# Second mixer: keys and queries projected pair by pair around the third gated projection and the first attention

## The chip, the core and the metric

One core of one Trainium2 chip runs the whole program. The metric is the time of one execution on the device in microseconds (us). The engines are TensorE (PE in the rows, its weight loads PEld), VectorE (DVE), ScalarE (ACT), GpSimd (POOL) and SyncE (SP, which here only issues transfers). Each engine runs its own instructions strictly in order and waits on semaphores for the others.

## What is computed

Two sequences of 256 tokens (width 1024) go through two layers, each a mixer and a convolutional feed-forward part, each followed by a layer norm. The first layer's mixer is a neighbourhood attention with a spatial gate. The change is in the second layer's mixer, which joins latent attention (8 heads, here 4 pairs) with a gated 31-tap convolution over 512 channels (here 4 groups of 128):

```python
def latent_attention(c_q, c_kv, k_rope_in, q_norm_g, w_uq, kv_norm_g, w_ukv, cos, sin):
    q = (rmsnorm(c_q, q_norm_g) @ w_uq).reshape(B, S, MLA_HEADS, MLA_NOPE + MLA_ROPE)
    q_nope, q_rope = jnp.split(q, [MLA_NOPE], axis=-1)
    q_rope = apply_rope(q_rope, cos[:, None, :], sin[:, None, :])
    kv = (rmsnorm(c_kv, kv_norm_g) @ w_ukv).reshape(B, S, MLA_HEADS, MLA_NOPE + MLA_V)
    k_nope, v = jnp.split(kv, [MLA_NOPE], axis=-1)
...
        s = (jnp.einsum('bqhd,bkhd->bhqk', qn_i, k_nope)
             + jnp.einsum('bqhr,bkr->bhqk', qr_i, k_rope)).astype(jnp.float32) * scale
        p = jax.nn.softmax(s, axis=-1).astype(v.dtype)
        return jnp.einsum('bhqk,bkhd->bqhd', p, v)

def odd_mixer(...):
    h = x @ w_in
    c_q, c_kv, k_r, glu_a, glu_g = jnp.split(h, [o1, o2, o3, o4], axis=-1)
    c = latent_attention(c_q, c_kv, k_r, ...)
    d = glu_a * jax.nn.sigmoid(glu_g)
    d = jax.nn.silu(layernorm(dwconv(d, conv_w, conv_b), conv_ln_g, conv_ln_b))
    return jnp.concatenate([c, d], axis=-1) @ w_out
```

## The kernel before

All 512 tokens stay on chip. Every fp32 product with a weight is made of three fast matmuls: the weight is split into a rounded half `whi` (a cast on ScalarE, L109) and the rest `wlo` (a subtraction on VectorE, L111), and the activations likewise (L115, L116). All of these matmuls are issued by one helper, L95, so the rows are told apart by tile names.

`odd_mixer` is written as a row of calls, and a list scheduler, which works with estimated durations, turns them into the fixed order of each engine; the order of the calls sets the priorities. The calls are:

- `glu(i)`, i from 0 to 3: the gated projection of one channel group, 2 times 24 matmuls into two PSUM banks, then its gate: a sigmoid on ScalarE (L551), the product into `dpad` on VectorE (L554), and the first tap of the convolution. The 31 taps of a group are shared out: 1 + 20 on VectorE (`cacc`, L557 and L719, accumulating in a PSUM bank) and 10 as products on ScalarE (`pr`, L559 and L723) that GpSimd adds up (L724); L725 adds both halves. From group 2 on, the gate also reloads ScalarE's table for the exponential.
- `cproj()` and `chain()`: the latent vectors, their norms, transposed to `cT`.
- `kvproj()`: v for the four blocks of tokens (`v1`, 4 times 3 matmuls, copied by ScalarE), then k of the four pairs (`k1`, 4 times 3 matmuls, copied by ScalarE into `kT`).
- `qproj()`: for each pair 6 matmuls for the rope half (evacuated by VectorE, L655) and 6 for the plain half (by ScalarE, L661), into `qT`.
- `attend(p)`: for each of two sequences and two heads (16 such steps in all, four to a pair; a step is called a head below) the scores `s`, the row maximum (DVE L491), two exponentials with their sums (ACT L494), a reciprocal (DVE L497), the scaling (ACT L501; in the last pair DVE L503), four transposes `pt` on TensorE and their copy to `PTr` (ACT, in the last pair DVE, L510), then the product with V (`pv`) and its split into `mixT`.

The calls stand in the order `glu(0)`, `cproj`, `chain`, `glu(1)`, `kvproj`, `qproj`, `glu(2)`, `attend(0)`, `attend(1)`, `glu(3)`, `attend(2)`, `attend(3)`; then the output projection's first half (`op0`, `dn1` banks), the convolution's taps, its layer norm (transposes `ct`, statistics, `cnm`, transposes back `cb`), and the projection's second half.

The exponentials are written to a ring of two tiles `er`, which is four half tiles, taken from the pool of large activation tiles. A second pool, `tp`, has eight temporaries of 2 KB per partition, among them the gates' sigmoids.

Of the kernel before, what the change touches and what calls it, by code (L numbers as in the profile page):

```python
# [11 lines left out]
AF = mybir.ActivationFunctionType  # L12
# [3 lines left out]
P = 128  # L16
# [3 lines left out]
T = 512  # L20
# [29 lines left out]
def tile_encoder(ctx: ExitStack, tc: tile.TileContext, I, O):  # L50
# [17 lines left out]
    def act(shape, dt=F32, s="a"):  # L68
        return actp.tile(shape, dt, tag="act", name=nm(s))
# [7 lines left out]
    class Ring:  # L77
# [6 lines left out]
        def get(self):  # L84
            j = self.i % (2 * len(self.t))
            self.i += 1
            return self.t[j // 2][:, j % 2, :].rearrange("p (a k) -> p a k", a=2)

    def bank(pool, s="ps"):
        return pool.tile([P, 512], F32, tag="b", name=nm(s))  # L90
# [441 lines left out]
    def odd_mixer(xT):  # L532
# [40 lines left out]
        G = {"start": last_mm[0]}  # L573
# [63 lines left out]
        def qproj():  # L637
            cT = G["cT"]
            wq = G["wq"]
            ropeT = G["kr"][:, 1:2, 0:S].broadcast_to([P, 2, S])  # L640
            qT = G["qT"] = [act([P, 2, T], s="qT") for _ in range(4)]

            def qfeat(pool, c):
                ps = bank(pool, "q")
                for k in range(2):
                    wh, wl = wq[k][0][:, c * P:(c + 1) * P], wq[k][1][:, c * P:(c + 1) * P]
                    mm(ps, wh, cT[k][:, 0, :], k == 0, False)
                    mm(ps, wh, cT[k][:, 1, :], False, False)
                    mm(ps, wl, cT[k][:, 0, :], False, k == 1)
                return ps  # L650
            for p in range(4):
                ps = qfeat(pB, 4 + p)
                for h in (0, 1):
                    rows = slice(64 - 64 * h, 128 - 64 * h)
                    nc.vector.tensor_tensor(out=qT[p][rows, h, :].rearrange("p (s t) -> p s t", s=2),  # L655
                                            in0=ps[rows].rearrange("p (s t) -> p s t", s=2), in1=ropeT[rows],
                                            op=ALU.mult)
                ps = qfeat(pC, p)
                for h in (0, 1):
                    rows = slice(64 * h, 64 * h + 64)  # L660
                    nc.scalar.activation(out=qT[p][rows, h, :], in_=ps[rows], func=AF.Copy, scale=96 ** -0.5)  # L661

        def kvproj():
            cT = G["cT"]
            wkv = G["wkv"]
            V = G["V"] = [wp.tile([P, 2, 512], F32, tag="w", name=nm("V1")) for _ in range(2)]
            for t in range(NT):
                ps = bank(pB, "v1")
                gemm_tok([ps], cT[2], t, wkv[0], wkv[1], [slice(512, 1024)], True, True)
                nc.scalar.copy(out=V[t // 2][:, t % 2, :], in_=ps)  # L670
            kT = G["kT"]
            for p in range(4):
                ps = bank(pC, "k1")
                wh, wl = wkv[0][:, p * P:(p + 1) * P], wkv[1][:, p * P:(p + 1) * P]
                mm(ps, wh, cT[2][:, 0, :], True, False)
                mm(ps, wh, cT[2][:, 1, :], False, False)
                mm(ps, wl, cT[2][:, 0, :], False, True)
                for h in range(2):
                    rows = slice(64 * h, 64 * h + 64)
                    nc.scalar.copy(out=kT[p][rows, h, :], in_=ps[rows])  # L680

        def attend(p):
            if p == 0:
                G["ring"] = Ring(2, "er"), Ring(2, "PTr")
            er, PTr = G["ring"]
# [16 lines left out]
        kvproj()  # L702
        qproj()
        glu(2)
        attend(0)
        attend(1)
# [215 lines left out]
```

## Time and profile before

| | us |
|---|---|
| median of the three runs | 1104.36 (1104.05 to 1105.21) |
| the profiled execution | 1104.76 |
| its span, first to last instruction | 1102.9 |
| TensorE busy | 1082.3 |
| VectorE busy | 673.2 |
| ScalarE busy | 488.7 |
| GpSimd busy | 226.6 |

The profiled execution is one run of its own. Busy times are sums over the span and say nothing of single stages; a matmul's end is modelled, since matmuls overlap. The second mixer lies between about 555 and 727 us.

### The profile page before, as it was taken

The numbers are of one execution on the slowest core, as the hardware profiler recorded it, in microseconds if no ns is written. First come the engines' busy times: TensorE is split into PE (matmuls) and PEld (weight loads), VectorE is DVE, ScalarE is ACT, GpSimd is POOL, SyncE is SP. The second block draws the span as 40 slices with busy tenths as digits, with TensorE's granted clock in tenths as the row PEclk, the third lists the DMA queues.
The fourth block names the chain that finished last, engine by engine and source line by source line (L and its number), as shares of the span: only waits on it lengthen the run. The fifth ranks groups of instructions, "written<-read, shape, count | busy, mean of one in ns | idle before, by whom it ended". The sixth has DMA issues, their size and how long they took to land.

```text
span 1102.9 us, 13655 instructions
## 1 busy us (share of the span) xinstructions
PE 1082.3 (98%) x5210; PEld 900.8 (82%) x5210; DVE 673.2 (61%) x996; ACT 488.7 (44%) x783; POOL 226.6 (21%) x222
## 2 busy tenths in 40 slices
PE   9999999999999999999999979999999999999996
PEld 7888778988888888888898856899888888888885
DVE  5378955766565656422578999587665656542227
ACT  5436644544444444421266797355444444431110
POOL 0482001200000000005464661830000000000173
PEclk9999999999999999999999979999999999999999
DMA  7852223533333323645232104254333333222602
GB/s 256 244 141 77 60 103 107 163 105 96 96 96 96 96 96 99 206 166 180 80 122 58 38 20 153 66 172 122 100 96 96 96 96 96 96 96 96 215 34 76
DMA packets 36098, 124.21 MB, mean 113 GB/s; under 512 B 4289, under 2 KB 5057, under 8 KB 36033
## 3 DMA queue, kind: packets, MB, share of 16 engines
q1 hardware_dynamic: 28864, 100.05, 29.5%
q0 software_dynamic: 6448, 22.53, 6.0%
q8 instruction: 41, 0.67, 0.3%
q10 hardware_dynamic: 720, 0.75, 0.2%
q14 instruction: 25, 0.20, 0.1%
HBM read 113.88 MB, written 8.39 MB: 111 GB/s over the span
## 4 chain that ended last, share of the span: by engine, by line
PE 93%; DVE 3%; ACT 2%; issue 1%; DMA 0%; POOL 0%; POOLq 0%; DVEq 0%; ACTq 0%
PE up L95 44%; PE dn L95 29%; PE qk L95 4%; PE op L95 4%; PE glu L95 3%; PE v L95 2%; PE u L95 2%; PE s L95 1%; PE pv L95 1%; PE pt L508 1%; DVE cacc L719 1%; PE lnT L237 1%; DVE wlo L111 1%; DVE qT L655 0%; ACT er L494 0%
## 5 line engine op out<-in xcount | busy, mean ns | idle before, releaser
L95 PE MATMUL up<-xT,whi 128*128 128x512 f32 (+1 forms) x1536 | 439.9, 371 | 0.0
L111 DVE TENSOR_TENSOR wlo<-raw,whi 128x1024 fp32r<-128x1024 f32 (+1 forms) x174 | 238.8, 1374 | 297.4 <-ACT whi L109 296.1
L95 PEld LDWEIGHTS up<-xT,whi 128*128 128x128 f32 x1536 | 279.9, 188 | 49.9
L109 ACT CAST whi<-raw 128x1024 fp32r<-128x1024 f32 (+1 forms) x174 | 182.4, 1050 | 249.1 <-PE dn L95 132.6
L95 PE MATMUL up<-xT,wlo 128*128 128x512 f32 (+1 forms) x768 | 284.0, 372 | 0.0
L95 PE MATMUL dn<-whi,gT 128*128 128x512 f32 x704 | 217.4, 389 | 0.0
L95 PEld LDWEIGHTS up<-xT,wlo 128*128 128x128 f32 x768 | 144.4, 188 | 24.9
L95 PEld LDWEIGHTS dn<-whi,gT 128*128 128x128 f32 x704 | 132.0, 188 | 27.2
L95 PE MATMUL dn<-wlo,gT 128*128 128x512 f32 x352 | 136.9, 389 | 0.0
L186 POOL DMA_DIRECT2D xres<-xscr x12 | 6.5, 546 | 576.0 <-PE dn L95 576.0
L95 PEld LDWEIGHTS dn<-wlo,gT 128*128 128x128 f32 x352 | 66.1, 188 | 13.8
L115 ACT CAST gT<-cv 128x512 fp32r<-128x512 f32 x44 | 27.3, 620 | 111.6 <-DVE cv L782 111.6
L771 ACT ACTIVATE cv<-up,par 128x512 f32<-128x512 f32 x88 | 68.3, 776 | 0.0
L774 DVE SCALAR_TENSOR_TENSOR cv<-up,par,cv 128x510 f32<-128x510 f32 x88 | 65.8, 748 | 2.7
L781 ACT ACTIVATE cv<-cv 128x512 f32<-128x512 f32 x44 | 27.8, 632 | 85.2 <-DVE cv L774 85.2
L772 DVE SCALAR_TENSOR_TENSOR cv<-up,par,cv 128x510 f32<-128x510 f32 x88 | 65.4, 743 | 0.0
L719 DVE SCALAR_TENSOR_TENSOR cacc<-dpad,par,cacc 128x512 f32<-128x512 f32 x80 | 58.9, 750 | 1.1
L724 POOL TENSOR_TENSOR acc<-acc,pr 128x512 f32<-128x512 f32 x36 | 48.7, 1353 | 38.9 <-ACT pr L723 32.2
L116 DVE TENSOR_TENSOR gT<-cv,gT 128x512 fp32r<-128x512 f32 x44 | 30.4, 692 | 27.5 <-ACT gT L115 27.5
L95 PE MATMUL op<-whi,mixT 128*128 128x512 f32 x128 | 44.3, 402 | 0.0
L95 PE MATMUL dn<-whi,mixT 128*128 128x512 f32 x128 | 42.8, 394 | 0.0
L95 PE MATMUL glu<-xT,khi 128*128 128x512 f32 (+1 forms) x160 | 42.0, 349 | 0.0
(195 smaller groups left out, 1351.4 us busy)
## 6 DMA issues: line engine op xcount, KB each, us to landing
raw<-in_wup SPq DMA_DIRECT2D x88, 512.0 KB, 3.6
raw<-in_wdn SPq DMA_DIRECT2D x44, 512.0 KB, 3.5
raw<-in_wout SPq DMA_DIRECT2D x16, 512.0 KB, 3.7
xscr<-xres POOLq DMA_DIRECT2D x12, 512.0 KB, 3.7
xres<-xscr POOLq DMA_DIRECT2D x12, 512.0 KB, 4.4
raw<-in_wqk SPq DMA_DIRECT2D x8, 512.0 KB, 6.6
raw<-in_wglu SPq DMA_DIRECT2D x8, 512.0 KB, 3.8
raw<-in_wug SPq DMA_DIRECT2D x7, 512.0 KB, 3.6
```

The source lines that it names most:

```text
L95: last_mm[0] = nc.tensor.matmul(out=out, lhsT=lhsT, rhs=rhs, start=first, stop=last)
L109: nc.scalar.copy(out=hi[:, :n], in_=raw[:, :n])
L111: nc.vector.tensor_tensor(out=lo[:, :n], in0=raw[:, :n], in1=hi[:, :n].bitcast(F32), op=ALU.subtract)
L115: nc.scalar.copy(out=dst[:, 0, sl], in_=src)
L116: nc.vector.tensor_tensor(out=dst[:, 1, sl], in0=src, in1=dst[:, 0, sl].bitcast(F32), op=ALU.subtract)
L237: nc.tensor.transpose(self.banks[k // 2][:, (k % 2) * S + q * P:(k % 2) * S + q * P + P], x[:, k * P:(k + 1) * P], ident)
L719: nc.vector.scalar_tensor_tensor(out=a, in0=dpad[i][:, :, j:j + S], scalar=pc("cw", i * 32 + j), in1=a, op0=ALU.mult, op1=ALU.add)
L724: nc.gpsimd.tensor_tensor(out=a2, in0=a2, in1=pr, op=ALU.add)
L771: nc.scalar.activation(out=c, in_=pv, func=AF.Identity, scale=pc(fw, ch * 4 + 1), bias=pc(fw, ch * 4 + 3))
L772: nc.vector.scalar_tensor_tensor(out=c[:, :, 1:S], in0=pv[:, :, 0:S - 1], scalar=pc(fw, ch * 4), in1=c[:, :, 1:S], op0=ALU.mult, op1=ALU.add)
L774: nc.vector.scalar_tensor_tensor(out=c[:, :, 0:S - 1], in0=pv[:, :, 1:S], scalar=pc(fw, ch * 4 + 2), in1=c[:, :, 0:S - 1], op0=ALU.mult, o ...
L781: nc.scalar.activation(out=cg, in_=cg, func=AF.Silu)
```

## The change

`qproj` and `kvproj` are taken apart. `kqproj(p)` projects k and q of one pair, with the same matmuls and evacuations; `vproj()` is what is left of `kvproj`. The pairs 0 and 1 are projected ahead of v and of the third gated projection, the pairs 2 and 3 behind the first pair's attention. The exponentials are no longer written to the ring `er` but each to a new tile of the pool of temporaries (`Loose`). Nothing else is changed; line numbers move by 3 or 4.

```diff
+    class Loose:
+        def get(self):
+            return tmp([P, 512], s="e").rearrange("p (a k) -> p a k", a=2)
...
-        G = {"start": last_mm[0]}
+        G = {"start": last_mm[0], "qT": [None] * 4}
...
+        def kqproj(p):
+            cT, wkv, kT = G["cT"], G["wkv"], G["kT"][p]
             ropeT = G["kr"][:, 1:2, 0:S].broadcast_to([P, 2, S])
+            qT = G["qT"][p] = act([P, 2, T], s="qT")
+            ps = bank(pC, "k1")
...
+            for h in range(2):
+                rows = slice(64 * h, 64 * h + 64)
+                nc.scalar.copy(out=kT[rows, h, :], in_=ps[rows])
+            ps = qfeat(pB, 4 + p)
...
+            ps = qfeat(pC, p)
...
         def attend(p):
             if p == 0:
-                G["ring"] = Ring(2, "er"), Ring(2, "PTr")
-            er, PTr = G["ring"]
+                G["ring"] = Ring(2, "PTr")
+            er, PTr = Loose(), G["ring"]
...
         glu(1)
-        kvproj()
-        qproj()
+        kqproj(0)
+        kqproj(1)
+        vproj()
         glu(2)
         attend(0)
+        kqproj(2)
+        kqproj(3)
         attend(1)
         glu(3)
```

What the scheduler makes of it shows in the built order. In the rows of an order, `name<-operands` are tiles with their numbers, `x2` is two such instructions in a row; the after version's line numbers are 3 or 4 higher.

TensorE where the first scores stand (`s`; `glu_5193` and `glu_5194` are the fourth gated projection, L95 is every matmul). Before:

```order
L95 MATMUL glu_5193<-xT_4277,klo_3991 128x512
L95 MATMUL glu_5193<-xT_4282,khi_3989 128x512 x2
L95 MATMUL glu_5193<-xT_4282,klo_3991 128x512
L95 MATMUL glu_5193<-xT_4287,khi_3989 128x512 x2
L95 MATMUL s_5027<-kT_4684,qT_4884 128x256 x2
L95 MATMUL glu_5193<-xT_4287,klo_3991 128x512
L95 MATMUL glu_5194<-xT_4252,khi_3995 128x512 x2
L95 MATMUL glu_5194<-xT_4252,klo_3997 128x512
L95 MATMUL s_5028<-kT_4684,qT_4884 128x256 x2
```

After (`glu_4911` is the third gated projection, `v_788` the last block of v, `glu_5197` the fourth gated projection):

```order
L99 MATMUL v_788_4905<-whi_4568,cT_4682 128x512
L99 MATMUL glu_4911<-xT_4282,khi_3893 128x512 x2
L99 MATMUL glu_4911<-xT_4282,klo_3895 128x512
L99 MATMUL glu_4911<-xT_4287,khi_3893 128x512 x2
L99 MATMUL glu_4911<-xT_4287,klo_3895 128x512
L99 MATMUL s_4973<-kT_4684,qT_4838 128x256 x2
L99 MATMUL s_4974<-kT_4684,qT_4838 128x256 x2
L99 MATMUL glu_5197<-xT_4252,khi_3989 128x512 x2
```

The first scores have moved ahead of the whole fourth gated projection and of half of the q and k projections.

ScalarE around the fourth gate's sigmoid (`sig`). Before (`er_5018<-s_5027` and `<-s_5028` are the exponentials of the first two heads, `er_5019<-s_5063` of the third):

```order
L494 ACTIVATE er_5018,rs_5050<-s_5028,nmx_5048 128x256 x2
L501 ACTIVATE er_5018<-er_5018,ri_5053 128x256 x2
L551 ACT_TABLE_LOAD
L551 ACTIVATE sig_5243<-glu_5194 128x512
L510 COPY PTr_5022<-pt_5042 128x512
L559 ACTIVATE acc_705_4425<-dpad_4421,par 128x512
L723 ACTIVATE pr_4428<-dpad_4421,par 128x512 x2
L494 ACT_TABLE_LOAD
L494 ACTIVATE er_5019,rs_5071<-s_5063,nmx_5069 128x256 x2
```

After (`e_5158` belongs to the seventh head, `e_5174` to the eighth):

```order
L505 ACTIVATE e_5129<-e_5129,ri_5135 128x256 x2
L498 ACTIVATE e_5158,rs_5161<-s_5152,nmx_5159 128x256 x2
L113 CAST whi_5765<-raw_5763 128x1024
L119 CAST mixT_4972<-pv_5145 128x256
L505 ACTIVATE e_5158<-e_5158,ri_5164 128x256 x2
L514 COPY PTr_4968<-pt_5139 128x512
L498 ACTIVATE e_5174,rs_5177<-s_5153,nmx_5175 128x256
L555 ACT_TABLE_LOAD
L555 ACTIVATE sig_5247<-glu_5198 128x512
L498 ACT_TABLE_LOAD
L498 ACTIVATE e_5174,rs_5177<-s_5153,nmx_5175 128x256
```

The sigmoid has moved from behind the second head to the middle of the eighth.

VectorE around the fourth gate's product (`dpad_4421`). Before (`cacc_5015` holds the third group's taps, `cacc_5248` the fourth's):

```order
L497 RECIPROCAL ri_5053<-rs_5050 128x2
L719 SCALAR_TENSOR_TENSOR cacc_5015<-dpad_4418,par,cacc_5015 128x512 x2
L554 TENSOR_TENSOR dpad_4421<-glu_5193,sig_5243 128x2x256
L491 TENSOR_REDUCE nmx_5069<-s_5063 128x2
L719 SCALAR_TENSOR_TENSOR cacc_5015<-dpad_4418,par,cacc_5015 128x512
L557 TENSOR_SCALAR cacc_5248<-dpad_4421,par 128x512
L719 SCALAR_TENSOR_TENSOR cacc_5015<-dpad_4418,par,cacc_5015 128x512
L719 SCALAR_TENSOR_TENSOR cacc_5248<-dpad_4421,par,cacc_5248 128x512
L719 SCALAR_TENSOR_TENSOR cacc_5015<-dpad_4418,par,cacc_5015 128x512
```

After (`cacc_4965` holds the third group's taps, `acc_705` takes its sum, `cacc_5252` is the fourth's):

```order
L722 SCALAR_TENSOR_TENSOR cacc_4965<-dpad_4418,par,cacc_4965 128x512 x2
L115 TENSOR_TENSOR wlo_5369<-raw_5365,whi_5367 128x1024
L728 TENSOR_TENSOR acc_705_4425<-cacc_4965,acc_705_4425 128x512
L501 RECIPROCAL ri_5135<-rs_5132 128x2
L495 TENSOR_REDUCE nmx_5159<-s_5152 128x2
L115 TENSOR_TENSOR wlo_5761<-raw_5757,whi_5759 128x1024
L501 RECIPROCAL ri_5164<-rs_5161 128x2
L495 TENSOR_REDUCE nmx_5175<-s_5153 128x2
L115 TENSOR_TENSOR wlo_5767<-raw_5763,whi_5765 128x1024
L120 TENSOR_TENSOR mixT_4972<-pv_5145,mixT_4972 128x256
L558 TENSOR_TENSOR dpad_4421<-glu_5197,sig_5247 128x2x256
L501 RECIPROCAL ri_5180<-rs_5177 128x2
```

The third group's taps have all moved ahead of the fourth gate's product, and weight differences (`wlo`) stand in between.

## Rows read from the trace of the kernel before

**Rows 1.** The page: the span, and each engine's busy time and share.

```profile
span 1102.9 us, 13655 instructions
...
PE 1082.3 (98%) x5210; PEld 900.8 (82%) x5210; DVE 673.2 (61%) x996; ACT 488.7 (44%) x783; POOL 226.6 (21%) x222
```

**Rows 2.** Stretches: window, busy us per engine, granted clock, DMA share and GB/s.

```profile
645.00:650.00 5.00, 2.13 (x5) 1.23 (x5) 4.59 (x9) 4.97 (x11) 2.48 (x3) 0.50 0.01 2
650.00:655.00 5.00, 4.34 (x13) 2.42 (x15) 5.00 (x10) 5.00 (x14) 4.53 (x4) 0.50 0.02 3
655.00:660.00 5.00, 5.00 (x25) 3.56 (x22) 5.00 (x11) 4.65 (x14) 3.01 (x4) 0.70 0.00 0
```

**Rows 3.** TensorE in order of time: start, length, instruction, [idle before, releaser].

```profile
631.09 1.02 PE L95 MATMUL s<-kT,qT 128*128 128x256 f32 x4
...
647.50 2.07 PE L95 MATMUL s<-kT,qT 128*128 128x256 f32 x4 [6.20 <-ACT er L494]
...
689.97 0.60 PE L508 MATMUL pt<-ident,er 128*128 128x128 f32 x4
```

**Rows 4.** Longer stretches, columns as in rows 2.

```profile
621.99:646.41 24.42, 19.31 (x90) 15.93 (x88) 22.50 (x37) 20.78 (x36) 14.88 (x11) 0.96 0.15 43
...
598.67:690.57 91.90, 83.10 (x400) 63.47 (x398) 86.46 (x155) 75.77 (x171) 41.75 (x38) 0.93 0.24 75
690.57:726.97 36.40, 36.38 (x174) 29.39 (x175) 20.94 (x33) 13.87 (x20) 23.92 (x12) 1.00 0.30 94
```

**Rows 5.** The chain of waits: start, length, engine and instructions.

```profile
602.23 4.08 PE glu L95 x18
```

**Rows 6.** ScalarE in order of time, columns as in rows 3.

```profile
613.25 1.20 ACT L661 ACTIVATE qT<-q 64x512 f32<-64x512 f32 x2
...
621.99 0.60 ACT L551 ACTIVATE sig<-glu 128x512 f32<-128x512 f32 x1 [0.16 <-PE glu L95]
...
639.59 0.91 ACT L501 ACTIVATE er<-er,ri 128x256 f32<-128x256 f32 x2 [0.23 <-DVE ri L497]
640.51 1.28 ACT L551 ACT_TABLE_LOAD   x1
641.81 0.60 ACT L551 ACTIVATE sig<-glu 128x512 f32<-128x512 f32 x1
...
643.80 1.32 ACT L723 ACTIVATE pr<-dpad,par 128x512 f32<-128x512 f32 x2
...
646.43 0.47 ACT L494 ACTIVATE er<-s,nmx 128x256 f32<-128x256 f32 x1
...
647.34 1.04 ACT L109 CAST whi<-raw 128x1024 fp32r<-128x1024 f32 x1
648.28 0.59 ACT L510 COPY PTr<-pt 128x512 f32<-128x512 f32 x1
...
664.60 0.47 ACT L494 ACTIVATE er<-s,nmx 128x256 f32<-128x256 f32 x1
```

**Rows 7.** VectorE in order of time, columns as in rows 3.

```profile
602.53 9.46 DVE L719 SCALAR_TENSOR_TENSOR cacc<-dpad,par,cacc 128x512 f32<-128x512 f32 x12
...
634.05 0.68 DVE L491 TENSOR_REDUCE nmx<-s 128x2 f32<-128x512 f32 x1
...
642.44 0.69 DVE L554 TENSOR_TENSOR dpad<-glu,sig 128x512 f32<-128x512 f32 x1 [1.41 <-ACT sig L551]
...
648.15 4.04 DVE L719 SCALAR_TENSOR_TENSOR cacc<-dpad,par,cacc 128x512 f32<-128x512 f32 x6
...
661.26 1.23 DVE L111 TENSOR_TENSOR wlo<-raw,whi 128x1024 fp32r<-128x1024 f32 x1 [0.24 <-PE s L95]
...
663.72 0.41 DVE L116 TENSOR_TENSOR mixT<-pv,mixT 128x256 fp32r<-128x256 f32 x1
...
675.18 0.69 DVE L725 TENSOR_TENSOR acc<-cacc,acc 128x512 f32<-128x512 f32 x1
...
681.42 0.61 DVE L503 TENSOR_SCALAR er<-er,ri 128x256 f32<-128x256 f32 x2
```

More of the change, by code (lines that the diff above doesn't have):

```diff
@@ L635, in chain @@
                                                                 op1=ALU.subtract)
-        def qproj():
-            cT = G["cT"]
-            wq = G["wq"]
-            ropeT = G["kr"][:, 1:2, 0:S].broadcast_to([P, 2, S])
[L641 to L661, printed above, removed]
@@ L663, in kvproj, with qfeat @@
-        def kvproj():
-            cT = G["cT"]
-            wkv = G["wkv"]
+        def qfeat(pool, c):
+            cT, wq = G["cT"], G["wq"]
+            ps = bank(pool, "q")
+            for k in range(2):
+                wh, wl = wq[k][0][:, c * P:(c + 1) * P], wq[k][1][:, c * P:(c + 1) * P]
+                mm(ps, wh, cT[k][:, 0, :], k == 0, False)
+                mm(ps, wh, cT[k][:, 1, :], False, False)
+                mm(ps, wl, cT[k][:, 0, :], False, k == 1)
+            return ps
+        def kqproj(p):
+            cT, wkv, kT = G["cT"], G["wkv"], G["kT"][p]
+            ropeT = G["kr"][:, 1:2, 0:S].broadcast_to([P, 2, S])
+            qT = G["qT"][p] = act([P, 2, T], s="qT")
+            ps = bank(pC, "k1")
+            wh, wl = wkv[0][:, p * P:(p + 1) * P], wkv[1][:, p * P:(p + 1) * P]
+            mm(ps, wh, cT[2][:, 0, :], True, False)
+            mm(ps, wh, cT[2][:, 1, :], False, False)
+            mm(ps, wl, cT[2][:, 0, :], False, True)
+            for h in range(2):
+                rows = slice(64 * h, 64 * h + 64)
+                nc.scalar.copy(out=kT[rows, h, :], in_=ps[rows])
+            ps = qfeat(pB, 4 + p)
+            for h in (0, 1):
+                rows = slice(64 - 64 * h, 128 - 64 * h)
+                nc.vector.tensor_tensor(out=qT[rows, h, :].rearrange("p (s t) -> p s t", s=2),
+                                        in0=ps[rows].rearrange("p (s t) -> p s t", s=2), in1=ropeT[rows],
+                                        op=ALU.mult)
+            ps = qfeat(pC, p)
+            for h in (0, 1):
+                rows = slice(64 * h, 64 * h + 64)
+                nc.scalar.activation(out=qT[rows, h, :], in_=ps[rows], func=AF.Copy, scale=96 ** -0.5)
@@ L666, in kvproj, with vproj @@
+        def vproj():
+            cT, wkv = G["cT"], G["wkv"]
             V = G["V"] = [wp.tile([P, 2, 512], F32, tag="w", name=nm("V1")) for _ in range(2)]
@@ L670, in kvproj @@
                 nc.scalar.copy(out=V[t // 2][:, t % 2, :], in_=ps)
[L671 to L680, printed above, removed]
         def attend(p):
             if p == 0:
-                G["ring"] = Ring(2, "er"), Ring(2, "PTr")
-            er, PTr = G["ring"]
+                G["ring"] = Ring(2, "PTr")
+            er, PTr = Loose(), G["ring"]
             qT, kT = G["qT"][p], G["kT"][p]
```

## Prediction

> **What bounds the kernel now.** I read the page first, then the busy time of each engine by stretch, then each engine's instructions in order of time. TensorE is busy 1082.3 of 1102.9 us [rows 1], so a change can win only where TensorE waits or runs at its lower clock. The stretches show one such place, the second mixer's attention: TensorE is busy 2.13 of the 5 us from 645 to 650, and the granted clock in the three stretches from 645 to 660 is 0.50, 0.50 and 0.70 [rows 2]. The instructions name the wait: before the score at 647.50 TensorE sat idle for 6.20 us, released by the exponentials on ScalarE; the first score was at 631.09 [rows 3]. From 598.67 to 690.57 TensorE is busy 83.10 of 91.90 us [rows 4], 8.8 us idle, and the 9.5 us of work at half clock (an estimate: 2.13, 4.3 and 3 us of the stretches from 645 to 660) cost 4.7 more. So 13.5 us is the most to be won here. But the same row has VectorE busy 86.46 of 91.90 us: the softmax chain goes through ScalarE and VectorE, which also run the 31-tap convolution. From 690.57 to 726.97 TensorE is busy 36.38 of 36.40 us [rows 4]: there its inputs are in time.
>
> **Part 1, what moves on TensorE.** Nothing is added or removed but two markers of a tile ring. Ahead of the first score now stand 90 matmuls (24 of q for two pairs, 6 of k, 12 of v, 48 of the third gated projection); before, another 24 of q, 6 of k and 23 of the fourth gated projection stood there too. At 18 matmuls in 4.08 us [rows 5], 0.227 each, 90 take 20.4 us from 598.8: the first score starts at 619.2 and not at 631.09, 11.9 us sooner. The rope rows that it also needs were written by SP's queue long before; that costs nothing.
>
> **Part 2, ScalarE up to the eighth head.** From the third gate's sigmoid, now at 619.3 (before at 621.99), to the second exponential of the eighth head (e_5174) the order has: 3 table loads at 1.28; 2 sigmoids and a preload, 1.4; 10 convolution products at 0.65 (1.32 for two); 8 heads' exponentials at 0.91 (from 646.43 to 647.34); 7 scalings at 0.81 (0.91 less the overlap with the next); 6 copies of transposes at 0.48; 4 weight casts at 0.94 (from 647.34 to 648.28); 4 pairs of k or q half copies at 1.20; 2 casts a quarter as wide as the weight's, some 0.3 by estimate [rows 6]. That is 3.8 + 1.4 + 6.5 + 7.3 + 5.7 + 2.9 + 3.8 + 4.8 + 0.6 = 36.8, so 656.1 if it never waits. Before, ScalarE is busy 20.78 of 24.42 us from the third gate's sigmoid through the table load behind the fourth's [rows 4], 3.6 us of waiting. In the new order I find as many (for the scores behind the new k projection, for probabilities times V, for GpSimd's adds) and take 3.8: 659.9. Before, the eighth head's exponentials began at 664.60 [rows 6] and ended near 665. So of the 12 us that attention starts sooner, 5 are left here.
>
> **Part 3, where they go: the fourth gate.** The list has the fourth gate's sigmoid between the eighth head's two exponentials. Before, it stood behind the second head, and the gate's product on VectorE ran at 642.44 [rows 7]. Now that runs at about 658.1 (659.9 less an exponential and a table load), 15.7 us later, although its matmuls end sooner. The last channel group's 20 taps can't start ahead of it. Before, they alternated with the third group's and filled VectorE's waits: six in a row on two tiles took 4.04 us, 0.66 each, twelve on one tile 9.46, 0.79 each [rows 7]. Now the third group is used up near 648, and VectorE idles some 4 us up to 658 with only row maxima and weight differences to do. TensorE idles too: its last filler, the fourth pair's q projection, ends near 646, and up to 660 I count 9.5 us of waiting for exponentials and scalings. The longest, some 4 us, is for the bank that the eighth head's scores hold across the sigmoid and both table loads. The wait of 6.20 us isn't removed; it moves from 641 to 656.
>
> **Part 4, VectorE to the end of attention.** From the fourth gate to the sum that closes the convolution the order has: gate and first product, 1.4; 20 taps, half at 0.66 and half at 0.79, 14.5; 8 row maxima at 0.60 and 8 reciprocals at 0.09, 5.5; 3 differences at 0.33; 6 scalings at 0.26; a copy and the closing sum at 0.6; a weight difference at 1.13 [rows 7] (durations less the 0.1 that overlaps with the next): 26.2 us, dense to 684.3. It can't be dense, since each reciprocal waits for exponentials: with the idle share of before (5.4 of 91.9 us) it is 685.9, and following each wait I get 686.6 if TensorE keeps its full clock. The granted clock fell in the idle time that ended at 647.50 and was back at full in 655 to 660, with TensorE busy again [rows 2, 3]. 9.5 us of waiting in 13.5 should bring that once more; scores, transposes and products of twice the length between 660 and 670 make it 690.5. I take 688.5, between the two. The Trainium skill, page TensorE: Matmul & The Clock Gate, section HAM oscillation, says that matmul bursts with waits between them find the array throttled anew each time, which speaks against this change; the trace's one case agrees (0.50 behind the wait), and by that rule alone it is 690.5 and the time 2.0 us more than my sum.
> Attention's last transposes come 2.1 us later (a reciprocal, a copy, a difference, a scaling, four transposes): 690.6. Before, the last four started at 689.97 and ended at 690.57 [rows 3]. **Attention ends where it ended.**
>
> **Part 5, the tail.** Before, the sum that closed the convolution was at 675.18 [rows 7]; its normalisation ran under the last heads. Now it closes with attention. Eight of the sixteen transposes into the normalisation come after it, 0.9 us (0.60 for four, less overlap). The last products with V wait for a copy behind two statistics on VectorE (counted as the closing sum, same size): scaling done at 1.55 after that sum, then 1.2 + 0.1 + 0.6, against transposes done at 2.1: 1.4 us. And behind the transposes out of the normalisation no filler is left: from the last attention matmul ScalarE has a weight cast, two activations and a cast, 0.94 + 0.62 + 0.62 + 0.6 = 2.8, TensorE transposes for 0.9: 1.9 us. The remaining 60 attention matmuls cover the chain between. Sum 4.2 us; bounds 0.9 (both waits hidden) and 7 (the result's second half held back by two weight differences beside GpSimd's work).
>
> ScalarE's table switches are as many as before. The rows show 1.28 from the load at 640.51, the sigmoid at 641.81, and no gap ahead [rows 6]. The Trainium skill, page ScalarE: Activation LUTs, section What ACT_TABLE_LOAD costs, adds a drain of about 1.38 us to each switch; an estimate from that page puts the fourth gate 2.8 us later and the time at 1111.4. The rows show no such drain, and I leave it out.
>
> The exponentials' tiles now come from the pool of temporaries, with the same instructions on them; two one-column fills fewer are 0.1 us of VectorE, hidden. That costs nothing.
>
> **Sum.** Attention 0.0, tail +4.2. The profiled execution took 1104.76 us, 1.9 more than its span and 0.4 more than the median of the runs. 1104.36 + 4.2 = 1108.6.
>
> **The rivals.**
> (a) *Faster: the lists close up.* ScalarE never waits up to the eighth head (656.1, not 659.9) and VectorE runs dense to the end (26.2 us, not 30.4). Attention ends 8.0 us sooner; with the tail's 4.2 the time is 1100.6, and 1097.3 if the tail's waits of 3.3 are covered too. For it: the first heads now have the fourth projection and two pairs' q and k beside them. Against it: 3.6 of 24.4 us were waits before, with filler on both sides. It decides from the fourth gate at 654 or sooner.
> (b) *No change.* The clock holds: 686.6 + 2.1 - 690.57 = -1.9, with a tail of 0.9 to 4.2: 1103.4 to 1106.7, say 1105.
> (c) *Worse.* The clock falls and GpSimd's affine work slows the tail's weight differences: 690.5 + 2.1 - 690.57 = 2.0, with a tail of 7: 1113.4.
> (d) *The order doesn't change as the diff says.* It does; under 1 in 100.
>
> **How the numbers follow.** The forecast, with all from +2.3 to +7 us: 0.47. (c) and beyond: 0.12. (b): 0.22. (a): 0.19. About 0.2%, 2.2 us, is what a measurement of this kernel can tell from no change. Faster 0.19, same 0.22, slower 0.59. The range leaves out about 1 in 10 at each end, the better half of (a) and the far end of (c): 1099.5 to 1113.
>
> **What would show each step.** Right: the first score at 619 to 620; the fourth gate's sigmoid at 656 to 659, inside the eighth head; a wait of TensorE of about 4 us ahead of the second head of the third pair; VectorE idle some 4 us ahead of the fourth gate's product; the closing sum within 3 us of the last transposes; a lower granted clock between 650 and 670. Wrong: the closing sum by 682 (then it is (a)), TensorE busy throughout 646 to 660, or no wait of TensorE behind the last product with V. The program up to 598 and from the second feed-forward part on should keep its durations.

## The result: 1116.97 us, 12.6 us slower

The changed kernel took 1116.97 us (median of four runs, 1116.84 to 1117.52), the kernel before 1104.32 beside it (1104.05 to 1105.21): a ratio of 1.0114, 95% interval 1.0097 to 1.0132. The prediction was 1108.6, range 1099.5 to 1113.0. The sign was right; the loss is three times the forecast and lies outside the range.

The page of the profile after (its profiled execution took 1116.98 us), as in [rows 1]:

```profile
span 1115.2 us, 13652 instructions
...
PE 1087.0 (97%) x5210; PEld 903.5 (81%) x5210; DVE 672.8 (60%) x994; ACT 488.9 (44%) x783; POOL 224.5 (20%) x222
```

The span grew by 12.3 us: TensorE idles 28.2 us where it idled 20.6, and its same instructions are 4.7 us longer, which I read as time at the lower clock and in shorter bursts. VectorE and ScalarE are busy as long as before.

Stretches of after, columns as in [rows 2]:

```profile
645.00:650.00 5.00, 3.47 (x16) 2.21 (x14) 4.13 (x5) 4.90 (x12) 0.00 (x0) 1.00 0.38 107
650.00:655.00 5.00, 3.61 (x13) 1.82 (x13) 3.32 (x7) 4.96 (x11) 0.00 (x0) 0.55 0.45 116
655.00:660.00 5.00, 3.16 (x15) 2.21 (x11) 2.12 (x4) 4.72 (x10) 0.00 (x0) 0.77 0.67 202
660.00:665.00 5.00, 3.54 (x8) 2.84 (x9) 3.71 (x7) 4.99 (x13) 1.53 (x2) 0.57 0.00 0
665.00:670.00 5.00, 5.00 (x25) 3.50 (x24) 2.95 (x7) 2.72 (x8) 4.98 (x8) 0.75 0.52 188
...
740.00:745.00 5.00, 3.01 (x14) 2.81 (x15) 4.54 (x17) 4.29 (x9) 2.98 (x1) 0.76 0.84 303
```

TensorE of after in order of time, columns as in [rows 3]:

```profile
618.97 1.89 PE L99 MATMUL s<-kT,qT 128*128 128x256 f32 x8
...
661.46 2.07 PE L99 MATMUL s<-kT,qT 128*128 128x256 f32 x4 [3.30 <-ACT e L498]
...
693.45 1.04 PE L512 MATMUL pt<-ident,e 128*128 128x128 f32 x8
695.22 1.95 PE L99 MATMUL pv<-PTr,V 128*64 128x256 f32 x16 [0.74 <-DVE PTr L514]
...
709.28 0.50 PE L99 MATMUL op<-whi,mixT 128*128 128x512 f32 x1 [1.86 <-ACT mixT L119]
...
738.26 1.03 PE L241 MATMUL lnT<-ident,xres 128*128 128x128 f32 x8
739.05 0.48 PE L99 MATMUL dn<-whi,mixT 128*128 128x512 f32 x1
741.66 0.74 PE L99 MATMUL up<-xT,whi 128*128 128x256 f32 x4 [2.13 <-DVE xT L251]
742.72 0.58 PE L99 MATMUL up<-xT,whi 128*128 128x256 f32 x1 [0.33 <-DVE xT L253]
```

Attention starts 12 us sooner (618.97 against 631.09 in [rows 3]) and ends 3.9 us later (last transposes done at 694.49 against 690.57). The low clock of [rows 2] lies later, from 650 to 670. The last two rows have no counterpart before: the second feed-forward part's first matmul waits for its normalised input, and the clock falls behind that. In the kernel before that matmul started without a wait:

```profile
731.54 0.76 PE L95 MATMUL up<-xT,whi 128*128 128x256 f32 x5
```

Both traces have 3514 matmuls ahead of it, so the two starts can be compared: 741.66 - 731.54 = 10.1 us are lost by then and 2.2 behind it. Of the 10.1 the rows show 2.13 directly ahead and 0.74 + 1.86 in the tail; the other 5.4 are attention's. So the loss is, counted by TensorE's work, **5.4 in attention, 2.6 in the tail's waits, 4.3 at the start of the second feed-forward part**. Attention's 5.4 is more than the 3.9 us between the two ends, because 11 transposes of the convolution's normalisation (`ct`, `cb`), done by then in the kernel before, are still to come.

ScalarE and VectorE of after at the fourth gate, and VectorE at the close of the convolution, for comparison with [rows 6] and [rows 7]:

```profile
657.64 1.28 ACT L555 ACT_TABLE_LOAD   x1
658.93 0.60 ACT L555 ACTIVATE sig<-glu 128x512 f32<-128x512 f32 x1
659.54 1.28 ACT L498 ACT_TABLE_LOAD   x1
```

```profile
659.56 0.69 DVE L558 TENSOR_TENSOR dpad<-glu,sig 128x512 f32<-128x512 f32 x1 [2.70 <-ACT sig L555]
...
690.61 0.68 DVE L728 TENSOR_TENSOR acc<-cacc,acc 128x512 f32<-128x512 f32 x1
691.21 0.15 DVE L501 RECIPROCAL ri<-rs 128x2 f32<-128x2 f32 x1
691.28 0.67 DVE L514 COPY PTr<-pt 128x512 f32<-128x512 f32 x1
691.87 0.41 DVE L120 TENSOR_TENSOR mixT<-pv,mixT 128x256 fp32r<-128x256 f32 x1
692.20 0.60 DVE L507 TENSOR_SCALAR e<-e,ri 128x256 f32<-128x256 f32 x2
```

### The profile page after: what moved, and what is told of

Its sections match the earlier page's. It is cut to its first block, busy times and chain, and to the rows that moved or that the text cites. A ratio compares the mean times of both kernels' runs of the same rounds, so it can differ in the third digit from the quotient of the medians.

```text
span 1115.2 us, 13652 instructions
## 1 busy us (share of the span) xinstructions
PE 1087.0 (97%) x5210; PEld 903.5 (81%) x5210; DVE 672.8 (60%) x994; ACT 488.9 (44%) x783; POOL 224.5 (20%) x222
## 4 chain that ended last, share of the span: by engine, by line
PE 92%; ACT 4%; DVE 2%; issue 1%; POOL 1%; DMA 0%; POOLq 0%; DVEq 0%; ACTq 0%
PE up L99 43%; PE dn L99 28%; PE qk L99 4%; PE op L99 4%; PE glu L99 3%; PE v L99 2%; PE u L99 2%; PE pv L99 1%; PE s L99 1%; PE pt L512 1%; PE lnT L241 1%; ACT e L498 1%; PE q L99 1%; ACT e L505 1%; ACT whi L113 0%
## 5 line engine op out<-in xcount | busy, mean ns | idle before, releaser
L120 DVE TENSOR_TENSOR gT<-cv,gT 128x512 fp32r<-128x512 f32 x44 | 30.4, 691 | 27.5 <-ACT gT L119 27.5
```

What stands on the lines that cost most here:

```text
L120: nc.vector.tensor_tensor(out=dst[:, 1, sl], in0=src, in1=dst[:, 0, sl].bitcast(F32), op=ALU.subtract)
```

## The experiments

### Which half of the diff

The diff does two things: it moves projections, and it takes the exponentials' tiles from another pool. e1_ring is the changed kernel with the old ring, e2_loose the kernel before with the pool alone.

```diff
-            er, PTr = Loose(), G["ring"]
+            er, PTr = G["ring"]
```

> The changed kernel with one part undone: the exponentials are written to the ring of two tiles again; the new order of the projections stays. Theory A (late gate): the temporaries are handed out in the order in which the code is written, so that the fourth gate's sigmoid, written behind the second pair's attention, can't have its tile before the eighth head has taken its own; that lateness brings the whole loss. Then the sigmoid runs inside the fourth head, at 637 to 640 instead of 658.93, the convolution closes by 676 instead of 690.61, TensorE's waits of 1.86 us in the output projection and of 2.13 us ahead of the second feed-forward part are gone, and the time is 1100 to 1106 us. Theory B (late pairs): the copies of the third and fourth pair's q and k among the exponentials and the missing filler for TensorE bring the loss; then the time stays at 1113 to 1118 us though the gate is early.

> The kernel before with the other part alone: the exponentials go to the pool of temporaries, the projections stand where they stood. Theory A (late gate): the gate falls to the eighth head here too, near 665 us, the convolution closes after attention's last scaling, and the time is 1110 to 1120 us. Theory B (late pairs): without the moved projections there is no loss, 1103.5 to 1106 us.

| | exponentials in the ring | in the pool |
|---|---|---|
| old order of projections | 1104.46 (before) | 1115.13, ratio 1.0097 (1.0081 to 1.0112) |
| new order | 1104.13, ratio 0.9998 (0.9988 to 1.0007) | 1116.97, ratio 1.0114 (1.0097 to 1.0132) |

Theory A holds: the pool brings nearly the whole loss, in either order. The moved projections cost nothing with the ring, and gain nothing; TensorE then starts the second feed-forward part without a wait. The gate's product on VectorE, in e1_ring and then in e2_loose:

```profile
638.98 0.69 DVE L558 TENSOR_TENSOR dpad<-glu,sig 128x512 f32<-128x512 f32 x1 [1.09 <-ACT sig L555]
```

```profile
657.06 0.69 DVE L558 TENSOR_TENSOR dpad<-glu,sig 128x512 f32<-128x512 f32 x1 [2.42 <-ACT sig L555]
```

Is it the lateness of the gate, or the sharing of eight temporaries? e3_gate_first keeps the pool and moves one call; e4_nine_tmp keeps the calls and adds a temporary.

```diff
         attend(0)
+        glu(3)
         kqproj(2)
         kqproj(3)
         attend(1)
-        glu(3)
```

```diff
-    tp = ctx.enter_context(tc.tile_pool(name="tp", bufs=8))
+    tp = ctx.enter_context(tc.tile_pool(name="tp", bufs=9))
```

> The changed kernel with one call moved: the fourth gated projection is written behind the first pair's attention, ahead of the third and fourth pair's projections, so that its sigmoid's tile is asked for behind four exponential tiles and not eight; the exponentials stay in the pool of temporaries. Theory A (late gate): the gate runs inside the fourth head, and the time is within 2 us of the kernel with the ring, 1100 to 1106 us. Theory C (too few temporaries, eight shared by exponentials, sigmoids and casts): the waits for tiles stay, and so does the time, 1113 to 1118 us. Theory B (late pairs): 1113 to 1118 us as well.

> The changed kernel with nine temporaries instead of eight, as many as the eight heads of two pairs and the sigmoid take together. Theory A (late gate, by the order in which tiles are asked for): the sigmoid keeps its place inside the eighth head, and the time stays at 1113 to 1118 us. Theory C (too few temporaries): the sigmoid no longer waits for a tile and the time falls to 1100 to 1106 us.

e3_gate_first took 1106.38 us (ratio 1.0012, 1.0003 to 1.0022), with the gate's product at 638.04. e4_nine_tmp took 1116.86 (1.011, 1.0095 to 1.0125): a ninth temporary changes nothing, and in its built order the sigmoid stays inside the eighth head, with no wait of its own there. So the number of tiles isn't the matter, and the late gate is: with the gate early, the pool costs next to nothing. Why the pool makes the gate late is my reading: a pool hands its tiles out in the order in which the code asks, and `glu(3)` stands behind `attend(1)`, so that its sigmoid, high priority or not, can't be placed before the eighth head has asked for its tile. The sigmoid's place fits that in all three kernels with the pool and the old place of `glu(3)` (inside the eighth head in the changed kernel, e2_loose and e4_nine_tmp); no run shows what the scheduler itself goes by.

### The stall at the second feed-forward part

No step of the prediction had this. The first run moves two of the four weight differences that VectorE did ahead of the normalised input (`cast0` is that input's first cast); nothing is left out.

```diff
-        head = [load(0), load(1)]
+        head = [load(0)]
+        with tc.issue_after(cast0[0].ins) if l == 1 else nullcontext():
+            head.append(load(1))
```

> The changed kernel (exponentials in the pool), with the second pair of weight tiles of the second feed-forward part loaded and split only behind the first cast of its normalised input; nothing is left out. It asks what the wait of 2.13 us ahead of that part's first matmul and the lower clock behind it (0.76 in the stretch from 740 to 745) cost. Theory G (four weight differences stand ahead of that cast on VectorE, 735.5 to 741.3, the wait follows from them and the clock from the wait): the first matmul starts 1 to 1.5 us sooner, the clock holds, and the time falls by 2.5 to 5 us, to 1112 to 1114.5. Theory H (the wait is only passed on, to the third matmul's weights or to the next input tiles): within 1.5 us of the changed kernel, 1115.5 to 1118.

1115.82 us (ratio 1.0099, 1.0083 to 1.0114), 1.2 less than the changed kernel and inside theory H's range. The first matmul started at 738.56, the wait moved to the fourth (1.46 us), and the granted clock was still 0.66 from 740 to 745.

The second run closes the convolution sooner.

```diff
-            for j in range(1, 31 - NPOOL):
+            for j in range(1, 31 - NPOOL - (12 if i == 3 else 0)):
```

> The changed kernel, late gate and all, with 12 of VectorE's 20 taps of the last channel group left out, so that the convolution closes some 8 us sooner although the gate is as late as before; part of the convolution isn't computed. It parts the loss of 12.6 us in two. Theory K: of it 4.6 us are lost in attention (waits and the lower clock ahead of the late gate) and stay, and 7.7 us (TensorE's waits in the output projection, 2.6, and ahead of and behind the start of the second feed-forward part, 5.1) come from the late close and go: 1107.5 to 1110.5 us. Rival: the loss is all made before the gate, or the late part doesn't hang on the close: 1114 to 1118 us. Should GpSimd's affine work fall among the last scalings, they would show over 1 us each, and the run would say nothing.

1116.96 us (1.0118, 1.0102 to 1.0133), the time of the changed kernel. That is the range of the rival, and the run doesn't part the loss as meant: GpSimd's additions end at 684.2, so the convolution closed at 686.07, 4.5 us sooner and not 8. Even so the first matmul of the feed-forward part started at 738.56, 3.1 sooner, and that was given back there, in waits of 2.37, 0.53 and 1.2 us and a clock of 0.50 from 740 to 745. So the stall doesn't hang on the close alone. The run shows one thing more: with 12 taps less on VectorE and all ten products still on ScalarE, the last transposes of attention are done at 690.90 and not at 694.49, with the same 3302 matmuls up to there.

The third run changes TensorE's order. Behind the transposes `lnT` of the first sequence TensorE has 9 output projection matmuls before, 1 after (the row at 739.05).

```diff
-                    for k in self.g[1]:
-                        self.step(k, t, h, w[h])
+                    late = sink.last_t is not None and t == 3 and h == 1
+                    with tc.issue_after(sink.last_t.ins) if late else nullcontext():
+                        for k in self.g[1]:
+                            self.step(k, t, h, w[h])
```

Here `last_t` is the last of those transposes; the line that sets it is left out.

> The changed kernel, late gate and pool and all, with twelve matmuls of the output projection (the last block of tokens, second half) held behind the transposes lnT of the first sequence. In the changed kernel 1 matmul of it stands between those transposes and the second feed-forward part's first matmul, in the kernel before 9; with the hold it is 12, and two of the four weight differences move behind the casts. Nothing is left out. Theory L (the wait of 2.13 us ahead of that part and the lower clock behind it come from the missing cover): the wait goes, the clock stays at 1.00 from 735 to 750, and the time falls by 3 to 5 us, to 1112 to 1114. Theory M (the held matmuls leave the same wait ahead of the transposes, since TensorE then has nothing to do while the residual is normalised): within 1.5 us of the changed kernel, 1115.5 to 1118.

1112.37 us (ratio 1.007, 1.0053 to 1.0087): 4.6 less than the changed kernel, with the late gate left as it was. TensorE and then its stretches in e13_after_cover:

```profile
734.79 1.91 PE L242 MATMUL lnT<-ident,xres 128*128 128x128 f32 x16
739.27 0.76 PE L99 MATMUL up<-xT,whi 128*128 128x256 f32 x5
```

```profile
735.00:740.00 5.00, 5.00 (x35) 4.52 (x34) 5.00 (x11) 4.73 (x10) 2.12 (x3) 1.00 0.80 270
740.00:745.00 5.00, 5.00 (x44) 5.00 (x43) 5.00 (x12) 3.98 (x6) 2.72 (x4) 1.00 0.18 57
```

No wait, and the clock stays up. Theory L holds: the third part of the loss is missing cover. The hold also moves two weight differences behind the casts, as in e8_weights_behind, which alone gained 1.2 us and only passed the wait on; if the two add up, 3.4 of the 4.6 are the cover's. The built orders show the matmuls that used to stand there ahead of the transposes; that the scheduler spent them as filler while it expected the late convolution is my reading of them.

### Why starting 12 us sooner gains nothing

e1_ring starts attention as early as the changed kernel and ends where the kernel before ends. I left out 12 of VectorE's 40 taps of the last two groups, in e1_ring (e5) and in the kernel before (e7).

```diff
-            for j in range(1, 31 - NPOOL):
+            for j in range(1, 31 - NPOOL - (6 if i >= 2 else 0)):
```

> The question is why the kernel with the ring, whose first scores start 12 us sooner than those of the kernel before, ends attention at the same time. This is the kernel with the ring, with 6 of VectorE's 20 taps left out in each of the last two channel groups: 12 taps, at 0.65 to 0.79 us each some 8.5 us of VectorE, and part of the convolution isn't computed. Theory D (VectorE's list sets the end of attention): the time falls by 5 to 9 us, to 1095 to 1099. Theory E (ScalarE's list sets it): within 1.5 us of the kernel with the ring, 1102.5 to 1105.5. Theory F (each head's chain from score to transposes sets it, whatever the lists hold): the same, 1102.5 to 1105.5.

> The kernel before, with the same 12 taps of VectorE left out as in the kernel with the ring and fewer taps. Theory D (VectorE's list sets the end whenever attention starts): the time falls as much as there, to 1095 to 1099 us, and the earlier start is worth nothing even so. If instead the earlier start is worth what VectorE's full list had hidden, the kernel before gains less, 1100 to 1103 us, and the new order is the faster one once VectorE has room.

Both became slower than the kernels that they were made from, by 10.2 and 8.0 us: 1114.32 (ratio to before 1.0086, 1.0071 to 1.0101) and 1112.42 (1.0076, 1.006 to 1.0093). No theory had that. VectorE and then GpSimd in e5_ring_less_dve:

```profile
678.60 0.59 DVE L507 TENSOR_SCALAR er<-er,ri 128x256 f32<-128x256 f32 x2
...
680.28 0.67 DVE L495 TENSOR_REDUCE nmx<-s 128x2 f32<-128x512 f32 x1
680.87 4.55 DVE L507 TENSOR_SCALAR er<-er,ri 128x256 f32<-128x256 f32 x2
685.34 0.80 DVE L174 TENSOR_SCALAR cnm<-ct,mv,rstd 128x512 f32<-128x512 f32 x1
686.06 0.68 DVE L514 COPY PTr<-pt 128x512 f32<-128x512 f32 x1
```

```profile
680.56 10.41 POOL L198 TENSOR_TENSOR xres<-xres,rowg 128x1024 f32<-128x1024 f32 x4
```

GpSimd's affine work on the residual follows the convolution's last statistic. With the convolution closed at 665 it falls among the last heads, and there two scalings take 4.55 us instead of 0.59, each about as long as one GpSimd instruction (2.60 on average). What reads PSUM is not slowed: row maxima 0.67, copies 0.68. The Trainium skill, page SBUF — State Buffer, section SBUF: two separate sides, calls the ports that some of VectorE's instructions share with GpSimd an exclusive lock: one starts first, and "the other fully blocks". The rows agree: the two scalings took 2.20 and 2.43 us, and each ended 0.15 us behind the end of a GpSimd instruction (683.07 behind 682.92, 685.42 behind 685.27).

So I repeated both (e9 from e5, e10 from e7) with that work held behind the last scaling (`last_sc`, set where the scalings are issued).

```diff
-                    with tc.issue_after(last_pow[0].ins):
-                        sink.res.affine(range(NT))
+                    with tc.issue_after(last_sc[0].ins):
+                        sink.res.affine(range(NT), last_sc[0])
```

> With 12 VectorE taps fewer the kernel with the ring became 10 us slower, not faster: its convolution closed at 665.18, GpSimd's affine work on the residual, which follows the convolution's statistics, began at 680.56 among the last heads, and there two scalings by VectorE took 4.55 us instead of 0.58. This run is the same kernel (12 taps left out) with GpSimd's affine work held until the last head's scaling is done. Theory J (the scalings wait for GpSimd's instruction, and nothing else made it slow): the scalings take 0.6 us again and the time falls below that of the kernel with the ring: by 5 to 9 us if VectorE's list sets the end of attention (1095 to 1099), by less than 1.5 us if ScalarE's list or the chain of each head does (1102.5 to 1105.5). Rival: if leaving out the taps itself disturbed the order, it stays above 1110 us.

> The kernel before with the same 12 taps left out and the same hold on GpSimd's affine work. It says what the earlier start of attention is worth when VectorE has room. If VectorE's list alone sets the end, both come out alike, 1095 to 1099 us. If the earlier start is worth something then, this one is slower than the kernel with the ring, 1099 to 1103 us against 1095 to 1099. If ScalarE's list or the chain of each head sets the end, it is near the kernel before, 1102.5 to 1105.

1103.68 (0.9989, 0.998 to 0.9999) and 1104.57 us (1.0002, 0.9992 to 1.0011). Theory J holds: the scalings are back at 0.6 and the loss of 10 and 8 us is gone. Theory D falls: 8.5 us less on VectorE gain half a microsecond with the ring and nothing without.

ScalarE's products left out instead (e6), and then both (e14):

```diff
-            for j in range(32 - NPOOL, 31):
+            for j in range(32 - NPOOL + (6 if i >= 2 else 0), 31):
```

> The kernel with the ring, with 6 of ScalarE's products (and GpSimd's additions of them) left out in each of the last two channel groups: 12 products at 0.61 to 0.65 us, some 7.5 us of ScalarE and 15.8 of GpSimd, and part of the convolution isn't computed. Theory D (VectorE's list sets the end): 1102.5 to 1105.5 us. Theory E (ScalarE's list sets it): the time falls by 4 to 8 us, to 1096 to 1100. Theory F (the chain of each head): 1102.5 to 1105.5.

> The kernel with the ring, with 12 VectorE taps and 12 ScalarE products (with GpSimd's additions) of the last two channel groups left out together, and GpSimd's affine work held until the last scaling. Taps alone, so held, left the time at 1103.68 us, products alone made it 1101.78. Theory E (ScalarE's list sets the end of attention, VectorE follows): near the run without products, 1100.5 to 1102.5 us. Theory N (both lists are full, and taking off one only brings up the other): clearly less than either, 1094 to 1099 us. Theory F (the chain of each head): above 1102.5 us.

1101.78 (0.9974, 0.9964 to 0.9984) and 1100.22 us (0.9961, 0.9946 to 0.9976). 7.5 us off ScalarE gain 2.4, and 16 us off both lists 3.9; neither time lies in a range that was forecast for it. The 2.4 are won early: in e6 the fourth gate's product stands at 636.31 and not at 638.98, and the sum that closes the convolution at 673.52 and not at 676.28, so by these rows the products left out of the third group brought the gain, and those of the fourth next to nothing. e6 also takes 15.8 us off GpSimd, whose additions weren't left out alone. ScalarE's list counts more than VectorE's here, neither sets the end alone, and most of the 12 us isn't found in either. Even in e14_ring_less_both TensorE waits for scalings and exponentials behind 650 (1.83 and 1.44 us), its filler used up, and the clock is 0.50 from 655 to 660. What part of this is the length of each head's own chain stays open.

### Tries for a faster kernel

Four kernels that compute everything shift work in e1_ring: the first half's two weight differences of the output projection to GpSimd (e12); the third pair's scalings to VectorE (e15), that and nine products instead of ten (e16); the last pair's scalings to ScalarE (e17). A fifth has eleven products (e18). In e12 `pool` is true for those two weight differences alone.

```diff
-        nc.vector.tensor_tensor(out=lo[:, :n], in0=raw[:, :n], in1=hi[:, :n].bitcast(F32), op=ALU.subtract)
+        (nc.gpsimd if pool else nc.vector).tensor_tensor(out=lo[:, :n], in0=raw[:, :n], in1=hi[:, :n].bitcast(F32), op=ALU.subtract)
```

```diff
-            attention(p, score, G["V"], mixT[p], lambda ps, h, e: ps, er, PTr, p < 3, p == 3)
+            attention(p, score, G["V"], mixT[p], lambda ps, h, e: ps, er, PTr, p < 2, p == 3)
```

```diff
-NPOOL = 10
+NPOOL = 9
```

e17 has `True` in place of `p < 3`, e18 `NPOOL = 11`.

> A try at a kernel faster than both, everything computed: the kernel with the ring, with the two weight differences of the output projection's first half moved from VectorE to GpSimd, which is idle for half of attention. It takes 2.4 us off VectorE and some 5 us of GpSimd. If VectorE's list sets the end of attention: 1101.5 to 1103.5 us. If ScalarE's or the chain of each head does: 1103.5 to 1105 us. If GpSimd's two instructions hold up its additions, and so ScalarE's products behind them: above 1105 us.

> A try at a kernel faster than both, everything computed: the kernel with the ring, with the third pair's four scalings moved from ScalarE (0.81 us each, 3.2 in all) to VectorE (0.5 each). By the run without 12 products, 2.4 us faster for 7.5 us less on ScalarE, theory E (ScalarE's list sets the end of attention) gives 1 us, 1102.5 to 1103.8 us. If VectorE's list counts as much: 1104 to 1106 us. GpSimd's additions end ahead of these scalings, so that they shouldn't meet them.

> The same with one product per channel group moved from ScalarE and GpSimd to VectorE as a tap (nine products and 21 taps a group): another 2.5 us off ScalarE and 2.8 more on VectorE. Theory E (ScalarE's list sets the end of attention): 1101 to 1103 us. If VectorE becomes the bound by it: 1104 to 1108 us.

> A try at a kernel faster than both, everything computed: the kernel with the ring, with the last pair's four scalings on ScalarE (0.81 us each) like those of the other pairs, not on VectorE. In the stretch from 680 to 685 VectorE is busy 5.00 of 5 us there and ScalarE 2.25. If VectorE's list sets the end of the last pair: 1102 to 1103.5 us. If the longer step in each head's chain (0.3 us) and ScalarE's table load count as much: 1104 to 1106 us.

> The opposite of the run with nine products: eleven products on ScalarE and GpSimd and 19 taps on VectorE a group, otherwise the kernel with the ring. Nine products and the third pair's scalings on VectorE made it slower, so that VectorE's list counts somewhere. If it counts more than ScalarE's: 1101.5 to 1103.5 us. If both lists are in balance and any shift costs: 1104 to 1106.5 us.

| | us | ratio to before |
|---|---|---|
| e12_ring_gpsimd_lo | 1108.60 | 1.0037 (1.0024 to 1.0050) |
| e15_ring_scale_dve | 1105.45 | 1.0011 (1.0002 to 1.0021) |
| e16_ring_scale_nine | 1106.48 | 1.0021 (1.0011 to 1.0030) |
| e17_ring_last_act | 1104.47 | 1.0001 (0.9992 to 1.0011) |
| e18_ring_eleven | 1108.88 | 1.0039 (1.0024 to 1.0054) |

None beats the kernel before. e15 and e16 speak against theory E alone: work taken off ScalarE and put on VectorE costs. e17, the opposite for the last pair, changes nothing. e12 and e18 say nothing about the balance, since both shorten VectorE's list, close the convolution sooner, and bring the collision back. VectorE in e12_ring_gpsimd_lo, whose affine work starts at 686.51:

```profile
684.67 0.59 DVE L508 TENSOR_SCALAR er<-er,ri 128x256 f32<-128x256 f32 x2
...
686.61 4.77 DVE L508 TENSOR_SCALAR er<-er,ri 128x256 f32<-128x256 f32 x2
```

e18 has the same 4.77 at 688.02. In e1_ring the last scalings start at 688.94 and the affine work at 690.18: the margin is about a microsecond. These two with that work held weren't tried.

## Why the prediction was wrong, step by step

- **Part 1 was right**: first score at 618.97, forecast 619.2.
- **Parts 2 and 3 were right in mechanism and near in time.** The fourth sigmoid is inside the eighth head, at 658.93 (656 to 659 forecast), the gate's product at 659.56 (658.1), 1.5 late. VectorE idles ahead of it (busy 2.12 of 5 us from 655 to 660), TensorE's longest wait stands where forecast, 3.30 us for some 4. From 646 to 660 its waits come to 4.8 us, half of the 9.5 counted. The clock fell as taken from [rows 2, 3]. The table switch shows no drain: the load starts at 657.64, the sigmoid 1.29 later.
- **Part 4 failed: "Attention ends where it ended" was 3.9 us short.** By its own mark, the end of the last transposes, attention ended at 694.49 and not at 690.6. Up to 665 and from there to that mark, before and then after, columns as in [rows 4]:

```profile
598.67:640.84 42.17, 42.17 (x191) 35.05 (x190) 40.12 (x58) 33.88 (x60) 24.76 (x18) 1.00 0.24 63
640.84:665.00 24.16, 16.72 (x70) 10.58 (x68) 22.08 (x40) 23.23 (x56) 14.59 (x15) 0.72 0.12 41
665.00:690.57 25.57, 24.21 (x142) 17.84 (x142) 24.27 (x59) 18.66 (x58) 2.40 (x5) 1.00 0.36 127
```

```profile
598.67:637.00 38.33, 37.94 (x175) 31.37 (x174) 34.77 (x56) 31.08 (x63) 23.25 (x18) 1.00 0.12 28
637.00:665.00 28.00, 21.11 (x84) 14.51 (x83) 21.09 (x33) 23.90 (x54) 1.53 (x2) 0.80 0.27 76
665.00:694.49 29.49, 25.69 (x133) 17.25 (x131) 26.22 (x52) 20.81 (x58) 13.14 (x14) 0.96 0.35 125
```

  Up to 665 TensorE idles 7.4 and 7.3 us: the waits have moved, as Part 3 says. Behind it TensorE idles 1.4 us before and 3.8 after. Part 4 named the right engine, VectorE, and its sum was too short. The closing sum ended at 691.21, forecast 688.5: the gate was 1.5 late, and VectorE's work from there was 27.5 us and not 26.2, with 4.1 us of waits for the 4.2 taken. About as much as the 1.3 us more stands in one place. Two scalings, 0.26 each in the sum, took 1.89 beside GpSimd's additions of the fourth group's products, which moved with the gate:

```profile
682.39 1.89 DVE L507 TENSOR_SCALAR e<-e,ri 128x256 f32<-128x256 f32 x2
```

```profile
681.50 2.63 POOL L727 TENSOR_TENSOR acc<-acc,pr 128x512 f32<-128x512 f32 x2 [0.79 <-ACT pr L726]
```

  That is the collision of e5_ring_less_dve in the changed kernel itself (e2_loose has the same 1.89 at 679.56). Behind the closing sum 1.2 us came on top: from 692.90 TensorE had thirteen transposes to do, five of the normalisation and eight of two heads, where the part counted four. e11_after_early_close agrees that VectorE sets this end: with 12 taps less attention ended at 690.90. The other list that got longer is ScalarE's, with the fourth group's ten products (6.5 us by the 0.65 of Part 2) among the heads of the last two pairs:

```profile
670.00:675.00 5.00, 4.24 (x26) 2.62 (x24) 4.37 (x9) 5.00 (x15) 1.78 (x2) 1.00 0.98 360
675.00:680.00 5.00, 3.58 (x15) 2.08 (x17) 4.87 (x10) 5.00 (x14) 1.83 (x2) 1.00 0.20 80
680.00:685.00 5.00, 4.16 (x25) 2.67 (x21) 4.96 (x9) 4.25 (x13) 3.87 (x4) 1.00 0.02 3
```

  ScalarE is full up to 680, and TensorE's waits there, 2.1 us, end on it; but e11_after_early_close has the same waits and ends early even so. No run took the products out alone, so their own share stays open.
- **Part 5 was right in size.** From the last transposes to the first matmul of the second feed-forward part it is 47.17 us after and 40.97 before, 6.2 more, and 2.13 of them are the wait ahead of that matmul: 4.1 us for the tail, forecast 4.2. The wait behind the last products with V was 1.86 (1.9 forecast), the one ahead of them 0.74 (1.4), and eight transposes into the normalisation did come behind attention. The bound of 7 didn't come: the two weight differences beside GpSimd took 5.54 us, but TensorE waited for ScalarE's half.
- **The sum ended too early.** "From the second feed-forward part on should keep its durations" put at nothing what cost 4.3 us by the rows, 4.6 by e13_after_cover; with attention's 3.9 it is the miss, and 3.9, 4.1 and 4.3 are the 12.3 us by which the span grew. The tail was said to be covered by the remaining matmuls. They were, and so, by my reading of the orders, they were missing for the next chain, the normalisation of the residual.
- **The rivals.** (a) rests on the lists closing up, which they did not, and (b) on the clock holding, which fell to 0.55. (c) had the fallen clock right and its second half, the tail's weight differences, wrong; at 1113.4 it too lacked the stall.
- **The pool at nothing.** "The exponentials' tiles now come from the pool of temporaries ... That costs nothing" is true of the instructions and false of the order: e2_loose shows 10.7 us for it alone. The prediction saw the late gate in the order, and priced it, but took it for a consequence of the moved projections, and so never asked what it would be without the pool.

## What to carry over

A tile pool is part of the order: here a sigmoid whose tile was asked for late in the code came late on the chip, so a change of pool can reorder as much as a change of calls. When filler is moved to cover one chain, look for the next chain that it used to cover, up to the point where the two orders have done the same work again. And finishing a side branch sooner isn't free: here an earlier close started GpSimd's work among VectorE's scalings and cost 8 to 10 us.

## What the runs showed of the hardware

- Two scalings of VectorE from SBUF to SBUF took 4.55 to 4.77 us beside GpSimd's two-input instructions of 2.6 us, 0.59 alone; VectorE's work on PSUM beside them kept its 0.67 and 0.68. Beside GpSimd's additions of 1.3 us two scalings took 1.89 (after, e2_loose).
- Behind a wait of 2.13 us ahead of the feed-forward part the granted clock was 0.76 in the stretch from 740 to 745, so for a part of it at its lower level. In e8_weights_behind it was 0.66 in the same stretch, behind a wait of 1.46 us. Behind the wait of 1.86 us ahead of 709.28 in the changed kernel it was 1.00 (705 to 715), and so it was with 3.8 us of idle time in waits of 1.0 us at most, from 670 to 690. What parts these cases the runs don't show.
